# Hybrid attention and delta-rule layer: v's copies loaded later, heads and merge reordered, a new order of the weight slabs

## The chip, the cores and the metric

The kernel runs on one core of a Trainium2 chip. The metric is device time in microseconds: the median of three runs of the whole program. The profile is one further execution, recorded by the hardware profiler.

## The reference

One layer of an encoder over 512 tokens of width 1024, all in float32:

```
h = RMSNorm(x);  one projection h @ w_in -> aq ak av az | dq dk dv db da dz | gate_att gate_dn
A: q, k = rope(norm(heads));  o = softmax(q k^T / sqrt(128)) v   (8 heads on 2 k/v heads)
   y_att = (o * silu(az)) @ w_br_att
B: dq, dk, dv through a 5-tap convolution and SiLU; gated delta rule in chunks of 64,
   forward and backward, summed, normalised per head, * silu(dz)
   y_dn = (...) @ w_br_dn
mix = (sigmoid(gate_att) * y_att + sigmoid(gate_dn) * y_dn) @ w_out
x = x + RMSNorm(mix);   e = p @ w_ple_proj
x = x + RMSNorm(sigmoid(x @ w_ple_gate) * e)
```

## The kernel before

**Tiling.** Every large matrix product is done as three 128x512 products of split operands: a float32 matrix is held as a rounded high part and a low part (the rest), and low·high, high·low and high·high are summed in PSUM. Weights come in *slabs* of 128 output columns: 1024 rows, 512 KB, loaded to a `wraw` buffer (two of them), rounded by ScalarE to `whi` (the cast at L122) and subtracted to `wlo` by GpSimd (L102) or VectorE (L97). There are two whi/wlo pairs. Units of the large SBUF buffer `u` that stand idle for a time can be lent as further raw buffers or pairs; the table SPARE says which unit, in what role, from and to which planned time. `gemm_t` (L546 to L548) multiplies one slab, 24 matmuls, into one of five PSUM banks `mm`; three more banks, `aux`, serve the small products. `kv`, `q0` and `q1` are wider blocks with the roles of the operands changed (`gemm_k`, L583 to L585). The slabs are named by their columns: dq, dk, dv (convolved), az and dz (SiLU gates), gA and gB (merge gates), each 0 to 7; ydn and yatt are the slabs of the two branch projections.

**Order.** A planner in Python (`Flow`) decides the order of all engines' instructions when the kernel is built: each job is a generator that yields what it waits for (an event, a buffer, a planned time) and gives each instruction a planned cost; priorities (`PR`) and the string `ORDER`, which lists the slabs, decide who is next. Each engine then executes its list strictly in order. All input DMAs go out on SyncE, also in order: `Q()` appends one, and a DMA that waits for its buffer holds those behind it.

**Delta branch.** It runs in two chains of four heads, g = 0 and 1. `phase_y` ends each chain: per head four transposes on TensorE (L1309) into a PSUM bank, a product by VectorE with the norm and the gate column, which comes back from DRAM by a DMA (`gi<-gate_dz`), a cast by ScalarE and a subtraction by VectorE, which give the split operand of the projection. The next head's transposes wait for that subtraction.

**Attention.** v is written to DRAM (`VD`) and copied back four times over into the partition groups of two units, 4 copies per unit (`v_rows`, L1505). `q_job` computes a half of q for all four row tiles, with a tail per tile; `q_done` frees q's unit and starts `att_heads(0)`. `att_heads(g)` (L1573) makes the scores of four heads (L1597 to L1599), exponentials, sums and transposes, and from L1635 the products with v in sixteen blocks of twelve matmuls, for each block one cast on ScalarE and one subtraction on VectorE (`blk<-u,blk` or `u<-u,u`). `scaled_gate` brings the inverse sums as a row (`gi<-SR`) and multiplies them into the gate on GpSimd. At the end each of four PSUM banks is multiplied by its gate and split into high and low parts: the operand `ya[g]` of the merge.

**Merge.** `yatt_two` (L1753) multiplies the first two yatt slabs, first with the four heads of group 0, then with those of group 1, in the order low·high, high·low, high·high for each head (L1769). `yatt_begin` loads the gate and the other branch's part, `yatt_tail` adds. The other six yatt slabs go through `gemm_t`; then come the output projection and the last gate.

Of the kernel before, what the change touches and what calls it, by code (L numbers as in the profile page):

```python
# [9 lines left out]
F32 = mybir.dt.float32  # L10
# [7 lines left out]
NT = 4  # L18
# [17 lines left out]
class Flow:  # L36
# [70 lines left out]
    def free(self, tag, t=None):  # L107
        self.slots[tag].append(self.now if t is None else t)
# [15 lines left out]
    def run(self):  # L124
        while self.parts:
# [31 lines left out]


ORDER = """
dq3 dk3 dk0 dq2 dk2 dq0 az0 dq1 dk1 az6 dv0 dv3 dz0 dq5 dv2 dq6  # L160
gA2 gB0 dk5 vec gA4 dv1 az7 gA6 az2 gA1 gB7 dq7 gB4 dq4 dk7 dz3
dk6 dk4 dz4 gA0 gA7 az5 dv5 dv7 gA5 dv6 dv4 gB3 gB6 dz5 gB5 kv
dz7 dz1 gA3 gB1 dz2 q0 dz6 gB2 q1 az4 az1 az3 free_h ydn6 ydn4 ydn2
ydn0 heads_on0 ydn7 ydn1 ydn5 ydn3 yatt0 yatt7 yatt5 yatt6 yatt1 yatt2 yatt3 yatt4 heads_on1 out0
out1 pg0 pg1
"""
OUT0 = 'yatt2 yatt7 yatt4 yatt5'
PR = dict(dec=4, dm1=7, y=6, conv=1, gate=8, kv=1, q=8, head=8, ple=9, prep=9, tab=1)
# [12 lines left out]
SPAREMM = 1
W1 = 0
COOL, HOT = 8.44, -2.1


@with_exitstack
def layer(ctx, tc, x, xT, pw0, wp1, wt, wba, wn, rows, qkn, hd16, npost, pnorm, dnorm, cs, out):
    nc = tc.nc
    pe, act, dve, pool, sync = nc.tensor, nc.scalar, nc.vector, nc.gpsimd, nc.sync

    caps = {"wraw": 2, "whi": 2, "wlo": 2, "f2": 5, "c2": 4, "blk": 3, "gi": 2, "go": 2, "mm": 5, "aux": 3}
    F = Flow({**caps, **{f"u{i}": 1 for i in range(17)}})
    op, free, spawn = F.op, F.free, F.spawn
# [127 lines left out]
    load, ple, late = {}, {}, {}  # L321
# [43 lines left out]
    first, second_ev, third = Event(), Event(), Event()  # L365
# [573 lines left out]
    def r32(i):  # L939
        return slice(32 * i, 32 * i + 32)  # L940
# [563 lines left out]

    def v_rows(g):  # L1505

        yield "at", max(late["VD", t] for t in range(NT)) - 0.5
        V4[g] = []
        for i, u in enumerate((15, 13)):
            yield "get", f"u{u}"  # L1510
            w = unit(u, [128, 8, 2, 128], F32R)
            V4[g].append(w)
            src = VD[g, 256 * i:256 * i + 256].rearrange("(b q) i n -> q b (i n)", q=32)
            for a in range(4):
                t = Q(2, late["VD", NT - 1], w[r32(a)].bitcast(F32).rearrange("p b i n -> p b (i n)"), src)
        return t

    def q_job(b, qus):
        if b == 0:
            late["q_tab"] = spawn(rope_tables(0), 4)  # L1520
        for u in qus:
            yield "get", f"u{u}"
        qbs[b] = tuple(unit(u, [128, 4, 512], F32R) for u in qus)
        o = yield from gemm_k(f"q{b}", hh, hl)
        for t in range(NT):
            att_ev[b, t] = spawn(q_tail(b, t, o[t]), PR["q"])
        if b == 1:
            spawn(q_done(), 4)

    def q_done():  # L1530
        for b in range(2):
            yield "ev", stat_ev["q", b]
            for t in range(NT):
                yield "ev", att_ev[b, t]
        free("u16")
        spawn(att_heads(0), PR["head"])
        att_start.set(F.now)
# [20 lines left out]
    def scaled_gate(h, te, uz_ev):  # L1558

        t = V(0.15, te, dve.reciprocal, rinv[:, 4 * h:4 * h + 4], sm[:, :, 2, h])  # L1560
        t = V(0.15, t, dve.transpose, rrow[h % 2], rinv)
        t = Q(0.2, t, SR[h].rearrange("t P i -> P t i"), rrow[h % 2])
        yield "at", t - 0.5
        yield "get", "gi"
        rb = tile("gi", [128, 512])
        t = Q(2, t, rb, row(SR[h, 4 * h:4 * h + 4].rearrange("t P i -> (t P i)"), 512))
        yield "ev", uz_ev
        uz = late["uz", h // 4, 0][:, h % 4, :]
        t = G(1.19, max(t, uz_ev.t), pool.tensor_mul, uz, uz, rb)
        free("gi", t)  # L1570
        return t

    def att_heads(g):  # L1573
# [44 lines left out]
        if g == 1:  # L1618
            free("u6")
        yield "ev", v_ev[g]  # L1620
        if g == 1:
            weighed.set(F.now)
        po = []
# [2 lines left out]
            yield "get", pb[a]  # L1626
            po.append(bank(pb[a], [128, 16, 32]))

        chains[0] += 1

        def pv(b, p):
            v = V4[g][b // 8][:, b % 8]
# [26 lines left out]
            yield "pe", PVB  # L1659
        for u in (15, 13):  # L1660
            free(f"u{u}")
        chains[0] -= 1
        for i in range(2):
            yield "get", f"ring{i}"
        free("u14")
# [8 lines left out]
            yield "ev", late["uz", h]  # L1674
        tz = [late["uz", h].t for h in range(4 * g, 4 * g + 4)]
        uz = late["uz", g, 0]
        for a in range(4):
            def at(w):
                return w.rearrange("p h (t a q) -> p (h t) a q", t=4, a=4)[:, :, a, :]
            if g == 0:  # L1680
                yield "get", "c2"
                y = tile("c2", [128, 16, 32])
                t = V(0.66, max(tz), dve.tensor_mul, y, po[a], at(uz))
                free(pb[a], t)
                yield "at", t
                th = A(0.55, t, act.copy, at(ya[g][0]), y)
                t = G(1.19, th, pool.tensor_sub, at(ya[g][1]), y, at(ya[g][0]).bitcast(F32))
                free("c2", t)
            else:
                t = V(0.66, max(tz), dve.tensor_mul, po[a], po[a], at(uz))  # L1690
                _, t = split(po[a], at(ya[g][0]), at(ya[g][1]), t, 512)
                free(pb[a], t)
        free("u16", t)
        head_ev[g].set(t + 0.2)
# [57 lines left out]

    def yatt_two(n1, n2):  # L1753

        o, need = {}, [head_ev[h // 4] for h in range(8)]
        for half in range(2):
            for n in (n1, n2):
                name = ("yatt", n)
                if half == 0:
                    o[n] = yield from yatt_begin(n)  # L1760
                    yield "ev", slab[name][0]
                    yield "get", "mm"
                    o[n] = bank("mm"), o[n]
                hi, lo = slab[name][1]
                for k in range(4 * half, 4 * half + 4):
                    if need[k].t is None or need[k].t > F.now:
                        yield "ev", need[k]
                    for w, y, first, last in ((lo, 0, k == 0, False), (hi, 1, False, False), (hi, 0, False, k == 7)):
                        pe.matmul(o[n][0], w[:, k, :], ya[k // 4][y][:, k % 4, :], start=first, stop=last)  # L1769
                    if k == 7:  # L1770
                        free(held["pair", name], F.now + 0.65)
                    yield "pe", 0.682
                if half == 1:
                    att_ev["mix", n] = spawn(yatt_tail(n, *o[n]), 5)
# [353 lines left out]
```

## Time and profile before

| | |
|---|---|
| three runs | 753.38, 754.19, 754.36 us (median 754.19) |
| the profiled execution | 754.32 us, span 752.6 us |
| TensorE busy | 728.9 us, 97% of the span, 4601 matmuls |
| VectorE, ScalarE, GpSimd busy | 494.6, 360.0, 301.6 us |
| chain that ended last, by engine | PE 80%, DVE 7%, DMA 5%, ACT 3%, POOL 3% |
| moved by DMA | 118.49 MB, mean 157 GB/s |

The span is the profiled execution without what lies around the program; 1.7 us lie around it here. Busy times are sums of instruction durations; for matmuls, which are pipelined, they are the time in which at least one is under way. PE is TensorE's matmuls and PEld its weight loads, DVE is VectorE, ACT ScalarE, POOL GpSimd, SP SyncE with its DMA queue SPq. In a row such as `gi<-gate_dz` the name ahead of the arrow is written, those behind it are read.

### The profile page before, as it was taken

The page shows a single profiled execution, that of the slowest core. Times are in us where ns is not written, and L with a number is a line of the kernel's source. Part 1 is how long each engine was busy: PE and PEld are TensorE (multiplying, and loading weights), DVE is VectorE, ACT ScalarE, POOL GpSimd, SP SyncE. Part 2 cuts the span into 40 slices and gives each one's busy share as a digit, 9 for nine tenths or more (in the row PEclk, how much of TensorE's full clock was granted, in tenths as well). Part 3 has the DMA queues.
Part 4 walks back from the last instruction along what each step waited for, and adds up shares of the span by engine and source line. Part 5 has one row for each costly group of instructions (what it writes and reads, how often), then busy time and mean ns, then how long its engine had stood idle before and what let it go on. Part 6 is the DMA issues. An engine that isn't in the chain of part 4 may idle for free.

```text
span 752.6 us, 12278 instructions
## 1 busy us (share of the span) xinstructions
PE 728.9 (97%) x4601; PEld 605.1 (80%) x4601; DVE 494.6 (66%) x907; ACT 360.0 (48%) x695; POOL 301.6 (40%) x288
## 2 busy tenths in 40 slices
PE   8999999999999999999999879999999979999995
PEld 7788888788888888888799758887778858788885
DVE  4687879887867758995945516277969873314434
ACT  6659573672653374434422243345647543332422
POOL 5836683112332443403402236472614536562501
PEclk9999999999999999999999998999999999999999
DMA  9854555775331344665402382425665756652323
GB/s 349 303 179 134 196 176 171 257 238 180 66 100 44 111 146 119 227 220 149 150 29 71 113 195 73 151 98 169 189 150 146 251 170 223 194 172 110 98 67 115
DMA packets 74732, 118.49 MB, mean 157 GB/s; under 512 B 23921, under 2 KB 39217, under 8 KB 74673
## 3 DMA queue, kind: packets, MB, share of 16 engines
q1 hardware_dynamic: 74384, 117.45, 49.7%
q8 instruction: 36, 0.59, 0.3%
q10 hardware_dynamic: 288, 0.26, 0.1%
q14 instruction: 24, 0.19, 0.1%
HBM read 93.41 MB, written 24.28 MB: 156 GB/s over the span
## 4 chain that ended last, share of the span: by engine, by line
PE 80%; DVE 7%; DMA 5%; ACT 3%; POOL 3%; issue 1%; SPq 0%; POOLq 0%; DVEq 0%; ACTq 0%
PE mm L546 15%; PE mm L548 14%; PE mm L547 14%; PE mm L565 4%; PE mm L567 4%; PE mm L566 4%; PE mm L583 2%; PE mm L584 2%; PE mm L585 2%; DMA gi<-gate_dz 2%; DMA wraw<-in_wt_dram 2%; PE aux L1215 2%; PE aux L1247 2%; POOL wlo L102 2%; PE aux L1233 2%; DVE blk L97 2%
## 5 line engine op out<-in xcount | busy, mean ns | idle before, releaser
L546 PE MATMUL mm<-u,wlo 128*128 128x512 f32 x496 | 200.1, 403 | 2.2 <-POOL wlo L102 1.4
L548 PE MATMUL mm<-u,whi 128*128 128x512 f32 x496 | 193.6, 390 | 0.0
L547 PE MATMUL mm<-u,whi 128*128 128x512 f32 x496 | 193.3, 390 | 0.0
L102 POOL TENSOR_TENSOR wlo<-wraw,whi 128x1024 fp32r<-128x1024 f32 x51 | 122.2, 2397 | 175.3 <-ACT whi L122 170.3
L546 PEld LDWEIGHTS mm<-u,wlo 128*128 128x128 f32 x496 | 93.3, 188 | 24.2 <-POOL wlo L102 2.8
L548 PEld LDWEIGHTS mm<-u,whi 128*128 128x128 f32 x496 | 93.1, 188 | 20.2
L122 ACT CAST whi<-wraw 128x1024 fp32r<-128x1024 f32 x66 | 69.1, 1047 | 82.4 <-PE mm L548 30.9
L547 PEld LDWEIGHTS mm<-u,whi 128*128 128x128 f32 x496 | 93.4, 188 | 16.9
L122 DVE SCALAR_TENSOR_TENSOR f<-mm,cw,f 128x510 f32<-128x510 f32 (+1 forms) x96 | 71.4, 746 | 9.0 <-ACT f L122 6.5
L102 POOL TENSOR_TENSOR u<-wraw,u 128x1024 fp32r<-128x1024 f32 x19 | 45.4, 2398 | 35.2 <-ACT u L122 35.1
L565 PE MATMUL mm<-u,u 128*128 128x512 f32 (+1 forms) x136 | 52.0, 383 | 0.0
L567 PE MATMUL mm<-u,u 128*128 128x512 f32 (+1 forms) x136 | 51.3, 378 | 0.0
L566 PE MATMUL mm<-u,u 128*128 128x512 f32 (+1 forms) x136 | 51.2, 377 | 0.0
L122 DVE TENSOR_TENSOR u<-aux,u 128x512 f32<-128x512 f32 (+2 forms) x55 | 35.8, 668 | 21.0 <-ACT u L122 12.6
L583 PE MATMUL mm<-whi,u 128*128 128x512 f32 x88 | 36.1, 410 | 0.0
L584 PE MATMUL mm<-wlo,u 128*128 128x512 f32 x88 | 35.1, 399 | 0.0
L585 PE MATMUL mm<-whi,u 128*128 128x512 f32 x88 | 35.1, 399 | 0.0
L122 ACT COPY c<-aux 128x512 f32<-128x512 f32 x18 | 10.6, 587 | 45.0 <-DVE f L122 35.5
L122 ACT ACTIVATE mm<-f 128x512 f32<-128x512 f32 x24 | 14.4, 601 | 34.5 <-DVE f L122 31.0
L567 PEld LDWEIGHTS mm<-u,u 128*128 128x128 f32 x136 | 25.6, 188 | 4.9
L566 PEld LDWEIGHTS mm<-u,u 128*128 128x128 f32 x136 | 25.6, 188 | 4.5
L565 PEld LDWEIGHTS mm<-u,u 128*128 128x128 f32 x136 | 25.6, 188 | 4.5
(280 smaller groups left out, 1467.2 us busy)
## 6 DMA issues: line engine op xcount, KB each, us to landing
wraw<-in_wt_dram SPq DMA_DIRECT2D x59, 512.0 KB, 3.7
wraw<-in_wn_dram SPq DMA_DIRECT2D x28, 512.0 KB, 4.2
u<-in_wt_dram SPq DMA_DIRECT2D x13, 512.0 KB, 5.2
u<-CI SPq DMA_DIRECT2D x16, 256.0 KB, 4.0
u<-VD SPq DMA_DIRECT2D x16, 256.0 KB, 6.9
u<-in_x_dram SPq DMA_DIRECT2D x4, 512.0 KB, 8.4
u<-in_xT_dram SPq DMA_DIRECT2D x4, 512.0 KB
eD<-u SPq DMA_DIRECT2D x8, 256.0 KB, 8.1
```

The lines of the kernel that those rows point to most:

```text
L97: self.shut = end, fn(*a, **k)
L102: ins = fn(*a, **k)
L122: fn(*a, **k)
L546: pe.matmul(o, lo[:, k, :], mh(k), start=(k == 0), stop=False)
L547: pe.matmul(o, hi[:, k, :], ml(k), start=False, stop=False)
L548: pe.matmul(o, hi[:, k, :], mh(k), start=False, stop=(k == 7))
L565: pe.matmul(o, b, hi, start=(i == 0), stop=False)
L566: pe.matmul(o, a, lo, start=False, stop=False)
L567: pe.matmul(o, a, hi, start=False, stop=(i == 7))
L583: pe.matmul(o[t], b, hi, start=(k == 0), stop=False)
L584: pe.matmul(o[t], a, lo, start=False, stop=False)
L585: pe.matmul(o[t], a, hi, start=False, stop=(k == 7))
```

## The change

Six things are changed; the arithmetic is the same, up to the order of sums in PSUM.

1. *v's copies.* `v_rows` waits for the event at the end of the second chain's phase_y, and for two planned microseconds (VGAP) ahead of each copy.
2. *First heads.* `q_done` runs once for each half of q. att_heads(0) is started when the tails of q0 are done (before: of both halves); its second part, and the second group, wait for q1's.
3. *scaled_gate* waits for its gate ahead of issuing the DMA of the sums, not behind it.
4. *Merge.* In the second group all four gate products and their casts come first, then the four subtractions. `yatt_two` puts the high parts of a group (low·high, high·high) ahead of its low parts (high·low); those of the second group are the last of all. `yatt_begin` moves to the second half.
5. *Idle units.* Unit 6 is lent as a pair for planned times 560 to 640, unit 14 as a raw buffer for 590 to 640; unit 13's loan ends at 480 instead of 525.
6. *The order string* and the planner's constants. `heads_on1`, the second group, stands ahead of the last two ydn slabs and of all yatt slabs; before, it stood behind all of them.

```diff
-dq3 dk3 dk0 dq2 dk2 dq0 az0 dq1 dk1 az6 dv0 dv3 dz0 dq5 dv2 dq6
+vec dq1 dk0 dk1 dk3 dq2 dk2 dq3 dq0 dv3 dv1 az0 dq5 dq7 dv2 dq6
...
-ydn0 heads_on0 ydn7 ydn1 ydn5 ydn3 yatt0 yatt7 yatt5 yatt6 yatt1 yatt2 yatt3 yatt4 heads_on1 out0
+ydn5 heads_on0 ydn6 ydn0 heads_on1 ydn1 ydn7 yatt6 yatt1 yatt5 yatt7 yatt4 yatt2 yatt3 yatt0 out0
...
-         (13, "pair", 443.0, 525.0))
+         (13, "pair", 443.0, SP13), (6, "pair", 560.0, 640.0), (14, "raw", 590.0, 640.0))
...
     def v_rows(g):
 
+        yield "ev", y_ev[1]
         yield "at", max(late["VD", t] for t in range(NT)) - 0.5
...
             for a in range(4):
-                t = Q(2, late["VD", NT - 1], w[r32(a)].bitcast(F32).rearrange("p b i n -> p b (i n)"), src)
+                yield "at", F.now + VGAP
+                t = Q(3, late["VD", NT - 1], w[r32(a)].bitcast(F32).rearrange("p b i n -> p b (i n)"), src)
...
-                t = V(0.66, max(tz), dve.tensor_mul, po[a], po[a], at(uz))
-                _, t = split(po[a], at(ya[g][0]), at(ya[g][1]), t, 512)
+                th = V(0.66, max(tz), dve.tensor_mul, po[a], po[a], at(uz))
+                th = A(0.55, th, act.copy, at(ya[g][0]), po[a])
+        if g == 1:
+            half_ev.set(th + 0.2)
+            for a in range(4):
+                t = V(0.58, th, dve.tensor_sub, at(ya[g][1]), po[a], at(ya[g][0]).bitcast(F32))
...
+        def lows(n, ks):
+            hi = slab["yatt", n][1][0]
+            for k in ks:
+                pe.matmul(o[n][0], hi[:, k, :], ya[k // 4][1][:, k % 4, :], start=False, stop=(k == 7))
...
+                for k in ks:
+                    for w in (lo, hi):
+                        pe.matmul(o[n][0], w[:, k, :], ya[half][0][:, k % 4, :], start=(w is lo and k == 0), stop=False)
+                    yield "pe", 0.455
+                if half == 0:
+                    lows(n, ks)
+                    yield "pe", 0.91
+        yield "ev", head_ev[1]
+        for n in (n1, n2):
+            lows(n, range(4, 8))
```

What this does to the order is shown at three places. The first is SyncE around q0 and q1. `gi<-gate_dz` is a gate load for phase_y, `<-VD` a copy of v, `wraw` a slab. Before:

```order
L122 DMA gi_4372<-gate_dz 128x512
L122 DMA gi_4405<-gate_dz 128x512
L122 DMA u_580_4430<-VD 32x8x256 x4
L122 DMA u_581_4431<-VD 32x8x256 x4
L122 DMA wraw_4461<-in_wt_dram 128x1024
L122 DMA gi_4491<-gate_dz 128x512
L122 DMA gi_4513<-gate_dz 128x512
```

Now:

```order
L122 DMA gate_dz<-go_4612 128x512
L122 DMA wraw_4704<-in_wn_dram 128x1024
L122 DMA gi_4715<-gate_dz 128x512
L122 DMA gi_4739<-gate_dz 128x512
L122 DMA wraw_4754<-in_wt_dram 128x1024
L122 DMA gi_4764<-gate_dz 128x512
L122 DMA wraw_4774<-in_wt_dram 128x1024
L122 DMA wraw_4811<-in_wt_dram 128x1024
L122 DMA u_643_4807<-VD 32x8x256 x2
L122 DMA wraw_4840<-in_wt_dram 128x1024
L122 DMA u_643_4807<-VD 32x8x256 x2
L122 DMA u_656_4867<-VD 32x8x256 x2
```

The eight copies of v moved behind the last gate load, in twos with slabs between them; the first row is the store of the gate column dz5, whose slab now stands between q0 and q1.

The second is TensorE behind the last product with v (L1635 before, L1645 now; `mm_6192` before and `mm_6012`, `mm_6144` now are banks of the first two yatt slabs). Before:

```order
L1635 MATMUL mm_5894<-blk_6114,u_743_5587 128x512
L1769 MATMUL mm_6192<-u_744_5588,wlo_6144 128x512
L1769 MATMUL mm_6192<-u_745_5589,whi_6143 128x512
L1769 MATMUL mm_6192<-u_744_5588,whi_6143 128x512
...
L1769 MATMUL mm_5923<-u_824_6184,wlo_5863 128x512
L1769 MATMUL mm_5923<-u_825_6185,whi_5862 128x512
L1769 MATMUL mm_5923<-u_824_6184,whi_5862 128x512
```

Now:

```order
L1645 MATMUL mm_5792<-blk_6070,u_761_5629 128x512
L1776 MATMUL mm_6012<-u_743_5548,whi_5848 128x512 x4
L1792 MATMUL mm_6144<-u_742_5547,u_787_5788 128x512 x8
L1776 MATMUL mm_6144<-u_743_5548,u_787_5788 128x512 x4
L1792 MATMUL mm_6012<-u_820_6138,wlo_5849 128x512
...
L1792 MATMUL mm_6144<-u_820_6138,u_787_5788 128x512 x8
L1776 MATMUL mm_6012<-u_821_6139,whi_5848 128x512 x4
L1776 MATMUL mm_6144<-u_821_6139,u_787_5788 128x512 x4
```

Sixteen matmuls that need only group 0 (u_742, u_743) now stand between the last product with v and the first use of group 1 (u_820, before u_824); before, it was twelve, all on the second slab's freshly split pair. The low part of group 1 (u_821, before u_825) is used last; before, second.

The third is VectorE at the same place. Before, from the two slab splits on:

```order
L97 TENSOR_TENSOR u_821_6142<-wraw_5861,u_821_6142 128x1024
L97 TENSOR_TENSOR wlo_6144<-wraw_5915,whi_6143 128x1024
L122 TENSOR_TENSOR aux_5891<-aux_5891,u_785_5810 128x512
L122 TENSOR_TENSOR aux_5892<-aux_5892,u_785_5810 128x512
L122 TENSOR_TENSOR u_825_6185<-aux_5891,u_824_6184 128x16x32
L122 TENSOR_TENSOR u_825_6185<-aux_5892,u_824_6184 128x16x32
L122 TENSOR_TENSOR aux_5893<-aux_5893,u_785_5810 128x512
```

Now:

```order
L97 TENSOR_TENSOR u_818_6110<-wraw_5970,u_818_6110 128x1024
L122 TENSOR_TENSOR aux_5789<-aux_5789,u_771_5682 128x512
L122 TENSOR_TENSOR aux_5790<-aux_5790,u_771_5682 128x512
L122 TENSOR_TENSOR aux_5791<-aux_5791,u_771_5682 128x512
L122 TENSOR_TENSOR mm_5792<-mm_5792,u_771_5682 128x512
L122 TENSOR_TENSOR u_821_6139<-aux_5789,u_820_6138 128x16x32
L122 TENSOR_TENSOR u_821_6139<-aux_5790,u_820_6138 128x16x32
```

One slab split stands ahead of the gate products instead of two, and the four products come in a row, the subtractions after them.

More of the change, by code (lines that the diff above doesn't have):

```diff
@@ L159 @@
 ORDER = """
-dq3 dk3 dk0 dq2 dk2 dq0 az0 dq1 dk1 az6 dv0 dv3 dz0 dq5 dv2 dq6
-gA2 gB0 dk5 vec gA4 dv1 az7 gA6 az2 gA1 gB7 dq7 gB4 dq4 dk7 dz3
-dk6 dk4 dz4 gA0 gA7 az5 dv5 dv7 gA5 dv6 dv4 gB3 gB6 dz5 gB5 kv
-dz7 dz1 gA3 gB1 dz2 q0 dz6 gB2 q1 az4 az1 az3 free_h ydn6 ydn4 ydn2
-ydn0 heads_on0 ydn7 ydn1 ydn5 ydn3 yatt0 yatt7 yatt5 yatt6 yatt1 yatt2 yatt3 yatt4 heads_on1 out0
+vec dq1 dk0 dk1 dk3 dq2 dk2 dq3 dq0 dv3 dv1 az0 dq5 dq7 dv2 dq6
+az5 gB7 dk5 az6 dz7 dk4 az2 gA2 dz2 gA4 gA6 dv0 gA7 dq4 dk6 gB4
+dk7 gA5 gB3 az4 dz1 dv7 dv4 dz6 dz0 gB0 gB1 kv dv5 dv6 gA0 dz4
+gB5 az3 az7 gB2 gA3 dz3 q0 dz5 gB6 q1 gA1 az1 free_h ydn3 ydn4 ydn2
+ydn5 heads_on0 ydn6 ydn0 heads_on1 ydn1 ydn7 yatt6 yatt1 yatt5 yatt7 yatt4 yatt2 yatt3 yatt0 out0
 out1 pg0 pg1
 """
-OUT0 = 'yatt2 yatt7 yatt4 yatt5'
-PR = dict(dec=4, dm1=7, y=6, conv=1, gate=8, kv=1, q=8, head=8, ple=9, prep=9, tab=1)
+OUT0 = 'yatt0 yatt3 yatt2 yatt7'
+PR = dict(dec=1, dm1=11, y=7, conv=1, gate=3, kv=9, q=5, head=6, ple=7, prep=1, tab=6)
 GAP = 0.0
-EXPS = 0.4
+EXPS = 0.32
+SP13 = 480.0
 SPARE = ((15, "raw", 7.0, 190.0), (11, "pair", 22.0, 80.0), (12, "pair", 22.0, 80.0), (14, "pair", 279.0, 375.0),
-         (13, "pair", 443.0, 525.0))
-EOUT = 22.91
+         (13, "pair", 443.0, SP13), (6, "pair", 560.0, 640.0), (14, "raw", 590.0, 640.0))
+EOUT = 29.73
 WIDE = 2.0
@@ L178 @@
 WARM = 5.5
-PVB = 0.75
+PVB = 0.695
+VGAP = 2.0
+HEADHOT = 1
 AHEAD = 4
-SPAREMM = 1
+SPAREMM = 2
 W1 = 0
-COOL, HOT = 8.44, -2.1
+COOL, HOT = 13.37, -0.27
 @with_exitstack
@@ L1526, in q_job, with q_done @@
             att_ev[b, t] = spawn(q_tail(b, t, o[t]), PR["q"])
[L1527 to L1537, printed above, removed]
+        spawn(q_done(b), 4)
+    def q_done(b):
+        yield "ev", stat_ev["q", b]
+        for t in range(NT):
+            yield "ev", att_ev[b, t]
+        q_ev[b].set(F.now)
+        if b == 0:
+            spawn(att_heads(0), PR["head"])
+            att_start.set(F.now)
+        else:
+            free("u16")
+    q_ev = [Event(), Event()]
     head_ev = {0: Event(), 1: Event()}
@@ L1541, in layer @@
     ya = [None, None]
+    half_ev = Event()
     def gates4(g):
@@ L1562, in scaled_gate @@
         t = Q(0.2, t, SR[h].rearrange("t P i -> P t i"), rrow[h % 2])
+        yield "ev", uz_ev
         yield "at", t - 0.5
@@ L1566, in scaled_gate @@
         t = Q(2, t, rb, row(SR[h, 4 * h:4 * h + 4].rearrange("t P i -> (t P i)"), 512))
-        yield "ev", uz_ev
         uz = late["uz", h // 4, 0][:, h % 4, :]
@@ L1578, in att_heads @@
             taken.set(F.now)
+            yield "ev", q_ev[1]
         T = unit(0, [128, 16, 4, 4, 32])
@@ L1620, in att_heads @@
         yield "ev", v_ev[g]
+        yield "ev", q_ev[1]
         if g == 1:
@@ L1627, in att_heads @@
             po.append(bank(pb[a], [128, 16, 32]))
-        chains[0] += 1
+        chains[0] += HEADHOT
         def pv(b, p):
@@ L1661, in att_heads @@
             free(f"u{u}")
-        chains[0] -= 1
+        chains[0] -= HEADHOT
         for i in range(2):
@@ L1676, in att_heads, with at @@
         uz = late["uz", g, 0]
+        def at(w):
+            return w.rearrange("p h (t a q) -> p (h t) a q", t=4, a=4)[:, :, a, :]
         for a in range(4):
-            def at(w):
-                return w.rearrange("p h (t a q) -> p (h t) a q", t=4, a=4)[:, :, a, :]
             if g == 0:
@@ L1753, in yatt_two @@
     def yatt_two(n1, n2):
-        o, need = {}, [head_ev[h // 4] for h in range(8)]
+        o = {}
+        def lows(n, ks):
+            hi = slab["yatt", n][1][0]
+            for k in ks:
+                pe.matmul(o[n][0], hi[:, k, :], ya[k // 4][1][:, k % 4, :], start=False, stop=(k == 7))
         for half in range(2):
@@ L1759, in yatt_two @@
                 if half == 0:
-                    o[n] = yield from yatt_begin(n)
                     yield "ev", slab[name][0]
                     yield "get", "mm"
-                    o[n] = bank("mm"), o[n]
+                    o[n] = bank("mm"), None
+                else:
+                    o[n] = o[n][0], (yield from yatt_begin(n))
                 hi, lo = slab[name][1]
[L1765 to L1774, printed above, removed]
+                ks = range(4 * half, 4 * half + 4)
+                yield "ev", (head_ev[0], half_ev)[half]
+                for k in ks:
[8 more added lines that the diff above has]
+            lows(n, range(4, 8))
+            yield "pe", 0.91
+            free(held["pair", ("yatt", n)], F.now)
+            att_ev["mix", n] = spawn(yatt_tail(n, *o[n]), 5)
     def yatt_job(n):
```

## The prediction

> **What bounds the kernel now.** I began with the page's busy times and the table of 20 us stretches (columns: stretch, its length, busy time of PE, PEld, DVE, ACT and POOL with counts, granted TensorE clock, DMA share, GB/s).
>
> ```profile
> span 752.6 us, 12278 instructions
> PE 728.9 (97%) x4601; PEld 605.1 (80%) x4601; DVE 494.6 (66%) x907; ACT 360.0 (48%) x695; POOL 301.6 (40%) x288
> ...
> 120.00:140.00 20.00, 19.69 (x87) 15.98 (x86) 18.16 (x33) 10.49 (x23) 4.73 (x5) 1.00 0.66 193
> 140.00:160.00 20.00, 20.00 (x90) 16.54 (x89) 18.56 (x31) 12.76 (x30) 2.05 (x4) 1.00 0.77 256
> 420.00:440.00 20.00, 17.25 (x91) 14.24 (x90) 9.17 (x20) 11.96 (x27) 8.48 (x7) 1.00 0.53 145
> 440.00:460.00 20.00, 15.63 (x62) 12.57 (x61) 3.98 (x6) 4.64 (x7) 6.30 (x3) 0.83 0.61 158
> 600.00:620.00 20.00, 15.60 (x149) 12.38 (x142) 15.15 (x23) 10.18 (x15) 5.12 (x3) 1.00 0.54 175
> ```
>
> TensorE is the bound: 728.9 of 752.6 us. Nothing in the change takes a matmul away, so a gain can only be TensorE's idle time, and that sits in two places: near 420 to 460, where the granted clock also drops to 0.83, and near 600 to 620. The table of waits names what ended those gaps (us in total, times, longest):
>
> ```profile
> PE mm L1309 <- DVE u L122: 5.9, 2, 4.4
> PE mm L1769 <- DVE wlo L97: 1.9, 1, 1.9
> PE mm L546 <- POOL wlo L102: 1.4, 2, 0.9
> PE mm L1769 <- ACT u L122: 1.3, 1, 1.3
> PE aux L1247 <- ACT c L122: 1.3, 1, 1.3
> PE mm L1769 <- DVE u L122: 0.2, 1, 0.2
> ```
>
> L1309 is the transposes of phase_y, L1769 the first two slabs of the merge. The chain that ended last (start, duration, what) shows who is behind the first; under it stand two rows of SyncE's issues from the timeline and the median landing times of such transfers.
>
> ```profile
> 425.91 5.31 DMA gi<-gate_dz
> ...
> 434.58 4.09 DMA u<-VD
> 438.74 9.52 DMA gi<-gate_dz
> ...
> 448.38 0.77 DVE mm L122
> 449.17 0.59 ACT u L122
> 449.79 0.70 DVE u L122
> ...
> 450.63 1.09 PE mm L1309 x4
> 451.72 0.43 PE mm L583
> ...
> 455.56 0.43 PE mm L583
> ...
> 456.34 0.23 PE mm L585
> ```
> ```profile
> 434.22 3.77 SPq L122 DMA_DIRECT2D u<-VD  x8
> 438.74 1.75 SPq L122 DMA_DIRECT2D gi<-gate_dz  x2
> ```
> ```profile
> u<-VD SPq DMA_DIRECT2D x16, 256.0 KB, 6.9
> gate_dz<-go SPq DMA_DIRECT2D x8, 256.0 KB, 2.5
> gi<-gate_dz SPq DMA_DIRECT2D x8, 256.0 KB, 4.8
> ```
>
> SyncE issues eight copies of v (8 x 256 KB, 2 MB) at 434.22; the two gate loads that phase_y needs stand behind them, go out at 438.74 and take 9.52 us where such a load has a median of 4.8. VectorE's product waits for the load until 448.38, and TensorE's next transposes for that product until 450.63. After this gap of 4.4 us the matmuls start 0.43 us apart for 451.72 to 456.34, against 0.23 before and after.
>
> The second place, from the timeline (start, us, engine, operation, in brackets the idle time before it and what ended it):
>
> ```profile
> 605.75 1.23 DVE L97 TENSOR_TENSOR u<-wraw,u 128x1024 fp32r<-128x1024 f32 x1 [1.12 <-ACT u L122]
> 606.89 1.22 DVE L97 TENSOR_TENSOR wlo<-wraw,whi 128x1024 fp32r<-128x1024 f32 x1
> 608.02 1.29 DVE L122 TENSOR_TENSOR aux<-aux,u 128x512 f32<-128x512 f32 x2
> ```
> ```profile
> 605.88 0.38 PE L1635 MATMUL aux<-blk,u 32*128 32x512 f32 x1
> 608.16 0.50 PE L1769 MATMUL mm<-u,wlo 128*128 128x512 f32 x1 [1.90 <-DVE wlo L97]
> ...
> 612.54 0.49 PE L1769 MATMUL mm<-u,wlo 128*128 128x512 f32 x1 [1.34 <-ACT u L122]
> ```
>
> When the last attention product ends (605.88 + 0.23, so 606.1), VectorE still owes two slab splits (1.2 us each), and only then the four gate products of the second head group, each followed by a cast and a subtraction. TensorE waits first for the split, then for the split heads.
>
> **The change, step by step.** I cost it against the profiled execution (754.32, span 752.6; the median of the three runs, 754.19, lies 0.13 below).
>
> *v's copies later and apart.* They now wait for the second chain's phase_y and stand behind all gate loads on SyncE. What goes is the wait of 5.9 us and the slow stretch: the transposes take 1.09 where four at full speed take half, so 0.5, and 451.72 to 456.34 is 4.62 us for some eleven matmuls that take 11 x 0.23 = 2.5: 2.1 us. Together 5.9 + 2.6 = 8.5 us. [...]
>
> The copies themselves are not needed before the attention products, some 40 us of matmuls later in the order; 6.9 us to land leave them hidden. The waits put ahead of them are waits of the planner, not of SyncE: nothing queues behind them.
>
> What is late next is the gate column dz5. By the new order its last product stands 14.5 us of TensorE's matmuls ahead of the point where VectorE wants its load (the order's matmuls at 0.227 us). VectorE gets to its multiply only after the four tails of q0.
>
> ```profile
> L122 DVE TENSOR_TENSOR c<-mm,u 128x512 f32<-128x512 f32 x10 | 6.8, 679 | 0.0
> ...
> L122 DVE TENSOR_TENSOR f<-mm,c 128x256 f32<-128x256 f32 (+1 forms) x24 | 8.0, 375 | 0.4
> ```
>
> A tail is two products (2 x 0.68), two half-size combinations (2 x 0.375) and about as much again as one product and a small sum: 3.0 us, an estimate. Four are 12 us; they begin 5.9 us of TensorE work before dz5's last product, so they end 6.1 after it; multiply 0.7, store 2.5, load 4.8: 14.1 of the 14.5 us there are. That is a tie. If the load takes 4.8, no wait; if it lands 1 us late, 0.8. I take 0.5. The PSUM bank of q1's fourth output, which the last of these tails frees, is as tight: 0 to 1.0, I take 0.3.
>
> *First heads after half of q.* att_heads(0) may start when q0's tails are done. Its work is not on the path, since q's matmuls fill TensorE; worth nothing by itself.
>
> *heads_on1 moved ahead of the last two delta-branch slabs and all merge slabs.* The second group's first attention product follows the last score after 6.8 us of other matmuls by the order. In between VectorE has to transpose the softmax and subtract the first weight block, behind whatever else stands in its queue. Ends: 0, if that fits in 6.8 us, and 1.4, if two instructions of 0.68 are too many. I take one, 0.7.
>
> *The merge.* After the last attention product TensorE has 4 + 8 + 4 matmuls that need only the first group: 16 x 0.227 = 3.6 us, to 609.7 on the old clock. VectorE has one slab split left instead of two, so its four products begin 1.13 us earlier (608.02 to 606.89), and at 0.6 us apart with 0.69 for the last they end at 609.4; the last cast (0.59 and 0.1 between) at 610.05. The wait is 0.3; if the split is done early 0, if it comes late as before 1.4. I take 0.4. Then sixteen high products, 3.6 us, cover the four subtractions (4 x 0.6 + 0.1 = 2.5). Gone: 1.9 + 1.3 + 0.2 = 3.4.
>
> *Idle units for slabs.* Two more buffers take a slab's block earlier, so the subtraction on POOL (2.4 us) starts earlier: the 1.4 us of L546 on POOL's wlo should go. Ends: all of it stays, or goes; I take that it goes, as each block gains about a slab of lead.
>
> Sum: 8.5 + 3.4 + 1.4 = 13.3 gone; 0.5 + 0.3 + 0.7 + 0.4 = 1.9 new. 754.32 - 13.3 + 1.9 = 742.9 profiled, 742.8 as a median. L1247's 1.3 us belongs to the chain that the order also moves; if it goes, and all new waits are 0, the low end is 754.2 - 13.3 - 1.3 = 739.6.
>
> **The rivals.**
>
> *A: dz5's gate comes really late.* In its tail the order puts slab transfers between the loads on SyncE; if one of those waits for POOL, the load goes out late, and a gap over 4 us with the half clock comes back. Price as before: 4.4 + 2.6 = 7.0 less the 0.5 counted: 749.3. For it: 14.1 of 14.5. Against: the two megabytes that made 9.52 of 4.8 are gone.
>
> *B: POOL holds VectorE in the second group's attention products.* Two rows of VectorE and one of POOL:
>
> ```profile
> 589.14 4.19 DVE L97 TENSOR_TENSOR blk<-u,blk 128x512 fp32r<-128x512 f32 x2
> ...
> 602.75 1.28 DVE L97 TENSOR_TENSOR u<-u,u 128x512 fp32r<-128x512 f32 x2
> ```
> ```profile
> 588.67 2.42 POOL L102 TENSOR_TENSOR wlo<-wraw,whi 128x1024 fp32r<-128x1024 f32 x1 [1.23 <-issue]
> ```
>
> Two subtractions of that stage took 4.19 us while POOL was in its wlo and in the gate products behind it, 1.28 where it was idle: 2.9 us more. There TensorE did not notice. In the new order this stage has sixteen subtractions, three splits and two gate products under 17.6 us of matmuls: 16 x 0.64 + 3 x 1.22 + 2 x 0.68 = 15.3 us. One such block makes 18.2, two make 21.1, 3.5 too many; less the 0.7 counted, 745.6. [...]
>
> *C: the denser start makes VectorE the bound, and the kernel slower.* Fourteen of the first fifteen column slabs are now convolution slabs, each with seven VectorE instructions under 24 matmuls (24 x 0.227 = 5.45 us).
>
> ```profile
> L122 DVE SCALAR_TENSOR_TENSOR f<-mm,cw,f 128x510 f32<-128x510 f32 (+1 forms) x96 | 71.4, 746 | 9.0 <-ACT f L122 6.5
> ```
>
> At 0.746 they take 5.2 us, just under. If POOL slows each by a third, to 0.99 us (the two subtractions above became 3.3 times as long), seven are 6.9, and fourteen slabs lose 14 x 1.45 = 20 us: 742.8 + 20 = 763. It ends slower than before from a mean of 0.90 us on ((5.45 + 11.4 / 14) / 7). Against: in 120 to 160 VectorE was busy 18.2 to 18.6 of 20 us, and TensorE 19.7 to 20.0. [...]
>
> *D: new waits of the same size.* The order of some 60 slabs changes; twelve microseconds of waits may open at places that I did not follow: 753 to 755.5. Against: slabs are matmuls of one kind that can change places, and of the 23.7 us that TensorE idled before (752.6 - 728.9) the six rows of waits hold 12.0. That the copies don't move is excluded by the order.
>
> **How the numbers follow.** A measurement of this kernel tells about 0.2% (1.5 us) from no change. Chances: forecast (739.6 to 744.5) 0.66, B 0.11, A 0.10, D 0.06, C 0.07. The time is the likeliest case's, 742.8. The range goes from 739.0 (the low end, and half a microsecond of the small waits) to 749.6 (A): it leaves out C, D and some of the edges, about 0.2. Faster: forecast, A, B, 0.87; same: most of D, 0.05; slower: C and the rest, 0.08.
>
> **What would show it.** Right: L1309 under 1 us of waits in all, granted clock 1.00 in every stretch between 20 and 740, gate loads near 5 us, L1792 and L1776 together under 1 us, no L546 behind POOL, TensorE busy near 727 in a span near 741. Wrong: a gap over 3 us before a transpose of phase_y (A), L1645 waiting for VectorE (B), TensorE below 19 of 20 us between 30 and 120 (C), or the sum of waits unchanged under other names (D).

## The result, and the profile after

The changed kernel took 746.87 us (median; 745.96 to 747.46), the kernel before 754.28 beside it: ratio 0.9902, 95% interval 0.9885 to 0.9919. It is faster by about 7.4 us, 11.5 were forecast; 746.87 lies in the range. The profiled execution took 745.96 us with a span of 744.2. From the page of the changed kernel, the span and the busy times:

```profile
span 744.2 us, 12250 instructions
PE 729.0 (98%) x4601; PEld 600.7 (81%) x4601; DVE 495.3 (67%) x912; ACT 348.8 (47%) x647; POOL 304.1 (41%) x292
```

TensorE's idle time fell from 23.7 us to 15.2 (744.2 - 729.0). Its busy time did not fall, although the stretch at half clock, 6.83 us of which 5.50 counted as busy, is gone. That is the first hint at what was left out. The stretches of the two places, and the one with the largest new wait (columns as before):

```profile
420.00:440.00 20.00, 20.00 (x114) 17.40 (x113) 8.75 (x23) 7.79 (x13) 8.97 (x8) 1.00 0.33 106
440.00:460.00 20.00, 20.00 (x96) 16.55 (x95) 10.01 (x18) 12.35 (x26) 13.19 (x12) 1.00 0.42 132
...
600.00:620.00 20.00, 20.00 (x116) 16.40 (x109) 11.48 (x17) 8.02 (x12) 5.44 (x3) 1.00 0.76 263
...
660.00:680.00 20.00, 18.61 (x87) 15.17 (x86) 7.05 (x8) 5.81 (x12) 8.43 (x8) 1.00 0.61 211
```

Both places are full and the clock is 1.00. TensorE's waits in the changed kernel, those above 0.5 us and those at the steps of the prediction (the first, 1.4 us, stands at the start of every kernel here):

```profile
PE mm L2017 <- POOL ident masks.py:199: 1.4, 1, 1.4
PE aux L1888 <- DVE whi L97: 1.4, 1, 1.4
PE mm L549 <- POOL wlo L102: 0.9, 1, 0.9
PE mm L1339 <- DVE u L97: 0.7, 1, 0.7
PE aux L1198 <- ACT c L122: 0.6, 1, 0.6
...
PE aux L1645 <- DVE u L97: 0.2, 1, 0.2
PE mm L1312 <- DVE u L122: 0.2, 1, 0.2
```

The transposes of phase_y (L1312) wait 0.2 us instead of 5.9; the merge (L1776, L1792) is not in the list at all. New is 1.4 us at L1888, the transposes ahead of the last gate.

The gate loads landed in 2.6 us (median) where they took 4.8, and the stores of the gate column in 3.6 where they took 2.5, as the list of DMA issues has it:

```profile
u<-VD SPq DMA_DIRECT2D x16, 256.0 KB, 6.8
gate_dz<-go SPq DMA_DIRECT2D x8, 256.0 KB, 3.6
gi<-gate_dz SPq DMA_DIRECT2D x8, 256.0 KB, 2.6
```

Behind the last product with v the merge runs without a gap (timeline, TensorE, then VectorE):

```profile
601.95 1.19 PE L1776 MATMUL mm<-u,whi 128*128 128x512 f32 x4
602.98 1.99 PE L1792 MATMUL mm<-u,u 128*128 128x512 f32 x8
604.81 1.07 PE L1776 MATMUL mm<-u,u 128*128 128x512 f32 x4
605.71 0.39 PE L1792 MATMUL mm<-u,wlo 128*128 128x512 f32 x1
```
```profile
600.24 1.23 DVE L97 TENSOR_TENSOR u<-wraw,u 128x1024 fp32r<-128x1024 f32 x1 [1.12 <-ACT u L122]
602.10 1.90 DVE L122 TENSOR_TENSOR aux<-aux,u 128x512 f32<-128x512 f32 x3 [0.63 <-PE aux L1645]
```

VectorE is done with the slab split before the last product with v ends, and its gate products wait for TensorE, no longer the other way round.

### The profile page after: what moved, and what is told of

Same layout as the page of the kernel before. It is cut to its first block, busy times and chain, and to the rows that moved or that the text cites. A ratio compares the mean times of both kernels' runs of the same rounds, so it can differ in the third digit from the quotient of the medians.

```text
span 744.2 us, 12250 instructions
## 1 busy us (share of the span) xinstructions
PE 729.0 (98%) x4601; PEld 600.7 (81%) x4601; DVE 495.3 (67%) x912; ACT 348.8 (47%) x647; POOL 304.1 (41%) x292
## 4 chain that ended last, share of the span: by engine, by line
PE 80%; DVE 8%; ACT 4%; DMA 3%; POOL 3%; issue 2%; POOLq 0%; DVEq 0%; SPq 0%; ACTq 0%
PE mm L549 14%; PE mm L550 14%; PE mm L551 14%; PE mm L570 4%; PE mm L568 4%; PE mm L569 4%; DVE f L122 3%; PE aux L1645 3%; PE mm L588 2%; PE mm L586 2%; PE mm L587 2%; PE aux L1218 2%; PE aux L1250 2%; PE aux L1236 2%; PE aux L1198 1%
## 5 line engine op out<-in xcount | busy, mean ns | idle before, releaser
L549 PE MATMUL mm<-u,wlo 128*128 128x512 f32 x488 | 197.2, 404 | 1.3 <-POOL wlo L102 0.9
L102 POOL TENSOR_TENSOR wlo<-wraw,whi 128x1024 fp32r<-128x1024 f32 x47 | 112.5, 2394 | 208.3 <-ACT whi L122 197.2
L551 PE MATMUL mm<-u,whi 128*128 128x512 f32 x488 | 190.4, 390 | 0.0
L550 PE MATMUL mm<-u,whi 128*128 128x512 f32 x488 | 190.2, 390 | 0.0
L549 PEld LDWEIGHTS mm<-u,wlo 128*128 128x128 f32 x488 | 91.8, 188 | 23.8 <-issue 4.0
L551 PEld LDWEIGHTS mm<-u,whi 128*128 128x128 f32 x488 | 91.6, 188 | 19.6
L550 PEld LDWEIGHTS mm<-u,whi 128*128 128x128 f32 x488 | 91.9, 188 | 16.4
L122 ACT CAST whi<-wraw 128x1024 fp32r<-128x1024 f32 x62 | 64.9, 1047 | 68.7 <-PE mm L551 28.3
L122 DVE SCALAR_TENSOR_TENSOR f<-mm,cw,f 128x510 f32<-128x510 f32 (+1 forms) x96 | 71.4, 745 | 6.6 <-ACT f L122 4.1
L102 POOL TENSOR_TENSOR u<-wraw,u 128x1024 fp32r<-128x1024 f32 x17 | 40.6, 2400 | 21.1 <-ACT u L122 21.0
L122 DVE TENSOR_TENSOR u<-aux,u 128x512 f32<-128x512 f32 (+2 forms) x55 | 36.1, 667 | 17.5 <-ACT u L122 11.7
L122 ACT COPY c<-aux 128x512 f32<-128x512 f32 x18 | 10.6, 587 | 48.1 <-DVE f L122 26.0
L586 PE MATMUL mm<-whi,u 128*128 128x512 f32 x80 | 31.8, 398 | 0.0
L588 PE MATMUL mm<-whi,u 128*128 128x512 f32 x80 | 31.2, 390 | 0.0
L587 PE MATMUL mm<-wlo,u 128*128 128x512 f32 x80 | 31.1, 389 | 0.0
L122 ACT ACTIVATE mm<-f 128x512 f32<-128x512 f32 x24 | 14.4, 600 | 32.2 <-DVE f L122 32.0
```

Source lines behind the costliest of these rows:

```text
L102: ins = fn(*a, **k)
L122: fn(*a, **k)
L549: pe.matmul(o, lo[:, k, :], mh(k), start=(k == 0), stop=False)
L550: pe.matmul(o, hi[:, k, :], ml(k), start=False, stop=False)
L551: pe.matmul(o, hi[:, k, :], mh(k), start=False, stop=(k == 7))
L586: pe.matmul(o[t], b, hi, start=(k == 0), stop=False)
```

## The experiments

Medians are over 4 to 12 executions; each ratio is to the kernel before, run beside it (753.8 to 754.3 us).

| kernel | us | ratio (95%) |
|---|---|---|
| before + late v | 752.58 | 0.9982 (0.9970 to 0.9994) |
| before + late v + unit 13 back at 480 | 747.28 | 0.9916 (0.9900 to 0.9933) |
| before + merge | 755.68 | 1.0021 (1.0012 to 1.0029) |
| before + merge + loans | 750.92 | 0.9958 (0.9946 to 0.9970) |
| before + all four | 744.88 | 0.9876 (0.9856 to 0.9896) |
| changed | 746.87 | 0.9902 (0.9885 to 0.9919) |
| changed, v early | 754.75 | 1.0013 (0.9998 to 1.0027) |
| changed, old merge | 749.39 | 0.9941 (0.9925 to 0.9956) |
| changed, last gate split on VectorE | 745.09 | 0.9890 (0.9874 to 0.9906) |
| changed, three blocks ahead | 743.42 | 0.9858 (0.9841 to 0.9876) |
| changed, both of these | 743.31 | 0.9858 (0.9838 to 0.9877) |
| changed, old column order | 753.96 | 0.9995 (0.9979 to 1.0010) |
| the same, three blocks ahead | 751.44 | 0.9968 (0.9956 to 0.9980) |

**v's copies.** The new `v_rows` alone, in the kernel before:

```diff
     def v_rows(g):
 
+        yield "ev", y_ev[1]
...
-                t = Q(2, late["VD", NT - 1], w[r32(a)].bitcast(F32).rearrange("p b i n -> p b (i n)"), src)
+                yield "at", F.now + VGAP
+                t = Q(3, late["VD", NT - 1], w[r32(a)].bitcast(F32).rearrange("p b i n -> p b (i n)"), src)
```

> The kernel before with the new v_rows alone (v's copies wait for the second chain's phase_y and go out apart). If the two megabytes ahead of the gate loads cause the wait at phase_y and the half clock behind it, both go: 754.3 - 8.5 = 745.8; the planner also packs the first group's products with v into one run here, which may give up to 1.9 us more (six single blocks at 0.31 us): 743.9 to 745.8. Rival: the gain at that place comes from the new slab order, and the gate loads stay late without it: 753 to 755.

It took 752.58 us: neither number. Its waits show that the mechanism holds and something else takes most of it back; under them stand the last issues of v's first set from the timeline of SyncE, and what VectorE waited for.

```profile
PE aux L1638 <- DVE blk L97: 4.7, 1, 4.7
...
PE mm L1310 <- DVE u L122: 1.8, 2, 1.5
PE aux L1638 <- ACT blk L122: 1.7, 1, 1.7
```
```profile
527.57 0.38 SPq L122 DMA_DIRECT2D u<-VD  x1
...
533.48 0.50 SPq L122 DMA_DIRECT2D u<-VD  x1
...
534.61 0.46 SPq L122 DMA_DIRECT2D u<-VD  x1
```
```profile
542.85 0.69 DVE L122 SCALAR_TENSOR_TENSOR go<-go,mm 128x512 f32<-128x512 f32 x1 [10.23 <-DMA wraw<-in_wt_dram]
```

The wait at phase_y (L1310 here) fell from 5.9 to 1.8 us. But half of v now went out at 527 to 535, among the slab and gate loads of that time; VectorE stood idle for 10.23 us until a slab load behind them had landed, with the subtractions of the first blocks behind it, and the products with v (L1638) waited 6.4 us; the granted clock was at half from 541.52 to 548.35. These copies go to unit 13, which is lent as a slab pair until 525. The change takes that loan back at 480, a constant that I had listed and not costed. So it was tried alone with it:

```diff
-         (13, "pair", 443.0, 525.0))
+         (13, "pair", 443.0, 480.0))
```

> The kernel before with the new v_rows and unit 13 given back at 480 instead of 525, nothing else. With v_rows alone the second half of v's copies went out at 527 to 535, since unit 13 was lent until 525, and the first products with v waited 4.7 + 1.7 us. If that loan is the whole of it, these waits go and phase_y's stay away: 753.9 - 5.9 - 2.6 + 1.8 (what was left at phase_y) = 747.2; 746 to 748. Rival: the products with v wait for ScalarE and VectorE in any case, since their queue was moved too: 751 to 753.

747.28 us, as expected: 0.2 us of the wait at L1638 are left, 1.8 us stay at phase_y. The profiled execution is the slowest of five (749.98; the fastest took 747.04); in it the clock is at half once more, from 607.93 to 611.34, behind the old merge's waits. The other way round, the changed kernel with the old `v_rows`:

> The changed kernel with the old v_rows. If v's copies are the cause, the gate load behind them is late again: 5 to 9 us more than the changed kernel's 746.9, so 752 to 756. Rival: the new slab order has taken the loads out of the way by itself: 746 to 748.

754.75 us, all of the gain gone. The load behind v's copies is late in the new order too. SyncE's issues, then VectorE's wait for the load and TensorE's:

```profile
442.96 5.09 SPq L122 DMA_DIRECT2D u<-VD  x8
448.99 0.34 SPq L122 DMA_DIRECT2D gi<-gate_dz  x1
```
```profile
458.76 0.76 DVE L122 SCALAR_TENSOR_TENSOR mm<-mm,dnn,gi 128x512 f32<-128x512 f32 x1 [12.08 <-DMA gi<-gate_dz]
```
```profile
PE mm L549 <- DVE u L122: 6.7, 1, 6.7
PE aux L1643 <- DVE blk L97: 2.1, 1, 2.1
```

Half clock follows here too, from 459.03 to 465.86. That settles the first place: the queue behind v's two megabytes makes the wait, in the old slab order and in the new one, and the copies can only go late where unit 13 is free.

**The merge.** `yatt_two` and the end of `att_heads` as changed, in the kernel before (the diff of both stands in the part on the change).

> The kernel before with the new merge alone (att_heads' products and casts first, yatt_two's high products first). If the order of the merge hides VectorE's work by itself: 3 to 3.5 us less, 750.8 to 751.3. Rival: the two slab splits still stand ahead of the gate products on VectorE, and the wait only changes its name: 753 to 754.3.

755.68 us: slower than before, by more than the rival said. The waits of the merge in this kernel, and TensorE around the longest:

```profile
PE mm L546 <- POOL wlo L102: 2.7, 1, 2.7
PE mm L1782 <- DVE wlo L97: 1.9, 1, 1.9
```
```profile
616.54 0.84 PE L1766 MATMUL mm<-u,whi 128*128 128x512 f32 x3
620.09 0.51 PE L546 MATMUL mm<-u,wlo 128*128 128x512 f32 x1 [2.71 <-POOL wlo L102]
```

The wait for the heads (1.3 us) is gone, but the low products, now last, read `whi`: the first slab keeps its pair until the end of the merge. ScalarE's cast for the next slab waits for that (timeline of ScalarE and of GpSimd):

```profile
616.55 1.05 ACT L122 CAST whi<-wraw 128x1024 fp32r<-128x1024 f32 x1 [3.62 <-PE mm L1766]
```
```profile
617.68 2.35 POOL L102 TENSOR_TENSOR wlo<-wraw,whi 128x1024 fp32r<-128x1024 f32 x1 [2.28 <-ACT whi L122]
```

Cast and subtraction then lie open, 2.7 us, and half clock follows, from 620.45 to 623.86. With the two loans:

```diff
-         (13, "pair", 443.0, 525.0))
+         (13, "pair", 443.0, 525.0), (6, "pair", 560.0, 640.0), (14, "raw", 590.0, 640.0))
```

> The kernel before with the new merge and the two loans (units 6 and 14), the second group's heads still behind all merge slabs. The merge alone came out slower, because the split of its second slab still stood ahead (1.9 us) and the next slab waited 2.7 us for its split on GpSimd. If the lent units are what it lacked: 1.9 + 1.3 + 1.4 less, 749.3; 748.5 to 750.5. Rival: the heads' new place in the order is needed as well, so that VectorE is free then: 752 to 755.

750.92 us, above the range that was expected. The wait of 2.7 is gone; 1.9 us stay, now for the split of a lent pair, since in the old place of the heads two splits still stand ahead of the gate products. The changed kernel with the old merge:

> The changed kernel with the old order inside the merge (product, cast and subtraction in turn; low parts second), loans and all else as changed. If the merge's order hides VectorE's chain: eight VectorE instructions instead of four stand ahead of the last high part, 4 x 0.6 = 2.4 us more, 749.3; 748.5 to 750. Rival: the loans did it, and the order inside the merge is worth under 1 us: 746.5 to 747.8.

749.39 us as expected, with the old wait for the heads back (`PE mm L1780 <- ACT u L122: 1.7`). That the number fits is in part luck: behind the wait the clock is at half from 609.35 to 612.76, which by an estimate (half of these 3.41 us) costs another 1.7 us and was not counted, and against it L1888's 1.4 us do not come in this order. New order of the merge and loans are one measure: the first frees VectorE and ties up a pair, the second replaces the pair.

**Do the two add up?** The kernel before with late v, unit 13, merge and loans, and with its own slab order:

> The kernel before with the late copies of v, unit 13 back at 480, the new merge and the two loans; the slab order, the heads' place and their start after both halves of q stay as before. If the two places are independent, the gains add: 753.8 - 6.6 - 2.9 = 744.3 (743.5 to 745.2), and then the rest of the change (the new slab order with what goes with it) costs some 2.5 us net. Rival: the rest of the change is needed for part of the gain, and this lands at 746 to 748, where the whole change does.

744.88 us: they add (6.6 and 2.9 were 9.5; it is 8.9). It is 2.0 below the whole change, at intervals that touch (0.9856 to 0.9896 against 0.9885 to 0.9919), so that the rest of the change shows no gain of its own and probably costs something. It is not without effect: this kernel still waits at its merge for the second split (`PE mm L1785 <- DVE u L97: 1.9`) and then runs 3.41 us at half clock (602.95 to 606.36), and the changed kernel does neither. So what the rest costs elsewhere is more than 2.0. Where, the next runs say.

**Attention products in runs.** In the changed kernel 15 of the 32 blocks of products with v stand alone between groups of three slab matmuls, 11 of them in the second group. The timeline of TensorE there:

```profile
584.56 0.39 PE L551 MATMUL mm<-u,whi 128*128 128x512 f32 x1
584.88 0.50 PE L1645 MATMUL aux<-u,u 32*128 32x512 f32 x3
...
585.21 0.40 PE L1645 MATMUL aux<-u,u 32*128 32x512 f32 x3
...
585.44 0.40 PE L1645 MATMUL aux<-u,u 32*128 32x512 f32 x3
...
585.78 0.50 PE L549 MATMUL mm<-u,wlo 128*128 128x512 f32 x1
586.11 0.40 PE L550 MATMUL mm<-u,whi 128*128 128x512 f32 x1
```

From one start to the next are 0.23 us where the form stays the same. At each change, from the 128-row matmul to the 32-row products and back, it is 0.32 to 0.34, and so is the next one behind it: 584.56 to 584.88 and 584.88 to 585.21 on the way in, 585.44 to 585.78 and 585.78 to 586.11 on the way out. These four together are 0.42 us more than 4 x 0.23. A block alone so costs 1.10 us with its two switches, where its products alone take 3 x 0.23 = 0.68; the run of twelve in this trace took 9.1 us, 0.76 each. Before, the 32 blocks stood in 9 runs, 7 of them of one block; now they stand in 17, 15 of one. Eight more runs at 0.42 are 3.4 us. None of this is idle time; it hides in TensorE's busy share. Each change so costs about 0.2 us in this trace, half of the 0.42; what TensorE does in that time is not seen in it.

The planner lets a slab's matmuls in because the next block must first get a buffer, which in the plan comes free 0.1 us after the block before. One block less in preparation removes that:

```diff
-AHEAD = 4
+AHEAD = 3
```

> The changed kernel with three instead of four blocks of weights prepared ahead in the attention products, so that TensorE takes them in runs of two to ten blocks and not one by one between slab matmuls: 7 runs instead of 17. In the trace of the changed kernel a single block of 12 takes 1.10 us with its switches, a block in a run 0.78. If the switching is part of the missing gain: 10 switches x 0.31 = 3.1 us less, 743.8. Rival: the blocks were apart because ScalarE and VectorE need the time; TensorE then waits at L1645 for them instead, and the time is 746 to 749.

743.42 us, 3.4 less, in 7 runs instead of 17. Ten runs fewer at 0.42 would be 4.2; one run of four in this trace, at 582.44, takes 0.9 us more than its products and switches. TensorE's busy time, from the page of this kernel, falls with it:

```profile
span 741.5 us, 12248 instructions
PE 725.7 (98%) x4601; PEld 602.5 (81%) x4601; DVE 491.3 (66%) x911; ACT 349.3 (47%) x647; POOL 306.9 (41%) x293
```

**The wait at L1888.** VectorE and GpSimd in the changed kernel:

```profile
673.03 2.85 DVE L97 SCALAR_TENSOR_TENSOR whi<-u,fs,whi 128x512 f32<-128x512 f32 x1 [0.42 <-POOL fs L306]
...
680.96 0.75 DVE L97 SCALAR_TENSOR_TENSOR whi<-u,fs,whi 128x512 f32<-128x512 f32 x1 [0.33 <-POOL fs L306]
```
```profile
672.97 2.37 POOL L102 TENSOR_TENSOR u<-wraw,u 128x1024 fp32r<-128x1024 f32 x1
```

The same instruction takes 0.75 us alone and 2.85 when GpSimd began a subtraction 0.06 us ahead of it: 2.10 more, near the 2.31 that were left of GpSimd's 2.37. The edit moves the splits of the last gate's weights to VectorE:

```diff
-            _, tl = split(raw, hi, lo, t, 1024, True, soon=name is names[0])
+            _, tl = split(raw, hi, lo, t, 1024, True, soon=name is names[0] or name[1] in ("pg0", "pg1"))
```

> The changed kernel with the low parts of the last gate's weights (pg0, pg1) subtracted by VectorE instead of GpSimd. In the changed kernel's trace one VectorE instruction with two SBUF inputs, 0.7 us elsewhere, took 2.85 beside such a subtraction on GpSimd (2.37), and TensorE's transposes behind it (L1888) waited 1.4. If GpSimd holds it up: 1.4 us less, 745.5. Rival: the transposes wait for the norm's chain over ScalarE and GpSimd, and VectorE's own splits get in its way: 746.9 to 748.

745.09 us, and L1888 waits for VectorE no more; VectorE's row takes 0.75 us in its trace. Its interval (0.9874 to 0.9906) overlaps that of the changed kernel, so that the 1.8 us are not shown by times alone; the profiled execution is the slowest of five (747.16), with waits elsewhere (1.1 at L1455, 1.5 at L549 behind GpSimd). Together with three blocks ahead:

> The changed kernel with three blocks ahead in the attention products and the last gate's weights split on VectorE. The runs of products gave 746.9 to 743.4. In that trace the collision at L1888 was already absent, so VectorE's splits should add nothing: 742.5 to 743.6. Rival: the collision comes and goes between executions and the 1.4 us are in the median: 742.0; other rival: VectorE's extra splits get in the way at the output: 744 to 745.

743.31 us, no different from 743.42: with the blocks in runs the two instructions miss each other anyway, and in the trace with three blocks ahead alone VectorE's row takes 0.75 us too (at 672.05). Both are faster than the kernel before by 10.4 us and than the changed one by 3.4, and stand as the best versions found.

**The column order.** The changed kernel with the first four rows of ORDER, those up to q1 and the last gate slabs, as before:

> The changed kernel with the old order of the column slabs (up to q1 and the last gate slabs); heads, merge, loans and v as changed. The new order shows more small waits up to 400 us than the old one (12.6 against 10.2 us over even spacing), but no 1.3 us at L1250 and 0.2 instead of 1.8 at phase_y's transposes. If these are all: 746.9 - 2.4 + 1.3 + 1.6 = 747.4, no difference (746.5 to 748). Rival: the new order is a plain loss: 744 to 745. Other rival: it is what makes the late copies work: 749 and more.

753.96 us, the other rival. Its waits do not lie where that rival had them, though:

```profile
PE mm L549 <- POOL wlo L102: 3.5, 4, 1.5
PE mm L549 <- DVE f L122: 2.5, 1, 2.5
PE aux L1236 <- DVE f L122: 2.1, 1, 2.1
```

Phase_y is not among them. The slabs wait for GpSimd's splits and for VectorE, the delta chain for VectorE, and half clock follows the wait of 2.5 us. It is not more work for GpSimd (300.6 us busy against 301.6 in the kernel before); the priorities and planned costs are the new ones. The old order was made with the old constants: order and constants were not separated here, so this says only that this order is no gain with these constants, not which order is better, and the cause stays open. With three blocks ahead:

> The changed kernel with the old order of the column slabs and three blocks ahead in the attention products (6 runs of products instead of 14). The switches go as before, 8 x 0.31 = 2.5 us less than the same with four blocks; if the old column order is no worse than the new: 743.5 to 745. Rival: the old order brings back the waits at phase_y and L1250: 746 and more.

751.44 us, 2.5 less, at intervals that touch. That is what eight runs fewer were to give by the 0.31 us of the expectation; at 0.42 it would be 3.4, and TensorE's busy time fell by that (730.3 to 726.9). The number is the rival's; of the waits that the rival named, phase_y is not in the list and L1250 has 0.7 us.

## Why the prediction was right, and where it was short

*v's copies.* Right in mechanism and nearly in size: 8.5 us were forecast, the wait fell from 5.9 to 0.2 and the half clock is gone. Taking the late copies out of the changed kernel costs 7.9 us (754.75 - 746.87). "They are not needed before the attention products" was right only because of unit 13's loan, which the step did not see: without that line the gain is 1.3 us. The slow matmuls that the step read, from 450.63 to 456.34, are the part of the slow stretch that lies behind the gap: the granted clock was 0.50 from 449.30 to 456.13, 6.83 us.

*dz5, the next to be late.* "That is a tie" held: the product waited for the load (5.91 us of VectorE's idle time, to 474.87), TensorE for 0.2. I took 0.5. It held because two errors cancelled: the store took 3.9 us for 2.5, and the load about 3.4 (471.46 to 474.87) for 4.8. The bank of q1's fourth output was not waited for, against 0.3.

*The second group's start.* 0.7 us were counted at L1645, 0.2 came. A wait of 0.9 stands just ahead instead, for a split that was queued on GpSimd behind the gate product, and that product behind its DMA.

*The merge.* 3.4 gone and 0.4 new were forecast; 3.4 went and nothing came, since the split on VectorE was early. Alone, without the loans, the new order was a loss, which the step did not say.

*The loans.* 1.4 were to go; 0.9 of that kind is still there, at another place.

*L1247.* The 1.3 us that only the low end counted did go; 0.6 at L1198 came in the same chain.

So idle time came out as forecast: 23.7 less 10.7 (5.9 + 3.4 + 1.4) and 1.9 more make 14.9, measured 15.2. In part that is luck: of the 1.9 only 0.4 came at the places named, and 1.4 came at L1888, which no step had. The step that failed is "a gain can only be TensorE's idle time" together with the item on `heads_on1`: I priced the second group's new place by the wait at its start alone. Its blocks now stand between slab matmuls, and that lengthens the matmuls: counted from each start to the next, the products with v kept TensorE busy for 24.3 us before, 26.1 now and 23.8 with three blocks ahead, the slab matmuls of `gemm_t` for 392.9, 394.6 and 393.1. Busy time was to fall by the 2.6 us of the half clock to 726.3 and stayed at 729.0; with the blocks in runs it is 725.7. These 2.7 us and 0.3 of idle time are nearly all of the 3.1 us by which the profiled execution (745.96) missed 742.9.

Of the rivals, A (a late dz5) and D (as many new waits) did not come. B came without its price: in the second group's attention products two subtractions took 2.38 us beside a gate product on GpSimd, 1.28 elsewhere, but TensorE waited 0.2 us for them; where GpSimd did cost time was L1888, 1.4 us. C did not come: no stretch between 40 and 200 us shows TensorE below 19.5. Of the signs of being right three failed: the gate loads came in 2.6 us and not near 5, 0.9 us behind a GpSimd split stayed, and TensorE was busy 729.0 us in a span of 744.2, not 727 in 741.

## What to carry to other kernels

A transfer moved out of the way of a queue needs its target free at the new time, and an order that reads an operand last holds that operand's buffer; look for the loan or the pair before costing the move. Two parts that each gain little or lose alone can be one measure. And where TensorE's busy time is nearly the whole span, count how often the form of its matmuls changes: here a block of products that stood alone took 0.42 us more with its two switches, all of it busy time, and no list of waits showed it.

## What the hardware showed unexpectedly

The clock fell to half after gaps far shorter than the 4.4 us of the kernel before: 2.5 us in the changed kernel with the old column order, 2.7 in the kernel before with the new merge (above), and 1.9 in the kernel before with all four. TensorE's row behind the first gap, then the slow stretches in this order, that of the kernel before last (columns as before; the clock is the third number from the end):

```profile
369.24 0.54 PE L549 MATMUL mm<-u,u 128*128 128x512 f32 x1 [2.51 <-DVE f L122]
```
```profile
369.50:372.91 3.41, 3.41 (x86) 2.40 (x89) 2.54 (x8) 0.00 (x0) 2.46 (x3) 0.50 0.35 119
...
620.45:623.86 3.41, 3.41 (x10) 2.67 (x9) 0.69 (x1) 1.12 (x2) 2.73 (x2) 0.50 0.63 191
...
602.95:606.36 3.41, 3.41 (x10) 2.63 (x9) 3.41 (x6) 3.08 (x5) 0.40 (x1) 0.50 1.00 365
...
449.30:456.13 6.83, 5.50 (x15) 4.56 (x16) 2.14 (x3) 1.99 (x3) 2.37 (x1) 0.50 0.26 79
```

In these traces the length of the gap alone does not decide it. Gaps of 2.1 us left the clock at 1.00, in the changed kernel with v early (its row of waits is above; the stretch) and with the old column order (425.91 to 428.02; 1.00 in the stretch from 420 to 440):

```profile
540.00:560.00 20.00, 17.93 (x220) 14.66 (x220) 17.27 (x24) 12.16 (x20) 6.03 (x3) 1.00 0.62 191
```

So did the 1.9 us at the merge of the kernel before (1.00 in the stretch from 600 to 620), while 1.7 us in the changed kernel with the old merge were followed by half clock, from 609.35 to 612.76. Directly ahead of the gap of 2.5 us ran 0.92 us of small 32x32 products. What decides whether the clock falls is not shown: no run moved a gap on purpose.

The wait of 2.7 us cost 4.3 in all: behind it the nine matmuls from 620.09 to 623.80 took 3.7 us where 9 x 0.23 is 2.1.
